# Whole modulation chunks, shift sums moved behind them, held-back sums lifted out at once, in a two-layer fp32 backbone

## The chip, the cores and the metric

The kernel runs on one core of one Trainium2 chip. The metric is the device time of one execution in microseconds, as the median of the runs: 2995.39 us over 3 runs (2994.27 to 2996.09).

## The reference, cut to what matters

Two layers work on 256 latent and 256 context tokens of width 2048, in fp32. Layer 0 mixes tokens by centred pooling, layer 1 by neighbourhood attention; behind each stands a gated MLP of inner width 5504 with a depthwise convolution of width 3. Only layer 0 up to its first MLP products is touched, and two norms later.

```python
def modulate(x, shift, scale):
    return x * (1 + scale) + shift

def conv_ffn(u, w_gate, w_up, conv_w, conv_b, w_down):
    gp = jnp.pad(u @ w_gate, ((0, 0), (1, 1), (0, 0)))
    gte = gp[:, :T] * conv_w[0] + gp[:, 1:T + 1] * conv_w[1] + gp[:, 2:] * conv_w[2] + conv_b
    return (jax.nn.silu(gte) * (u @ w_up)) @ w_down

def pool_mix(u, w, b, scale):          # 4 groups of 512 channels, windows 2, 4, 8, 16
    ...
    parts.append(window_sum / count[None, :, None] - ug)
    ...
    y = jnp.einsum('btgc,gcd->btgd', p, w).reshape(B, T, D) + b
    return y * scale
```

The shift, scale and gate of each sub-layer come from a product of SiLU(c) with a modulation matrix (2048 x 12288 a layer, for latent and context).

## The kernel before

**Precision.** Every fp32 weight tile is split into a high part (cast on ScalarE, line 172) and a low part (difference on VectorE, line 175); a product is three fp32r matmuls of 128x512, the 512 columns being both streams of 256 tokens.

**The four stages.** Layer 0 is worked in four groups g of 512 channels (lines 946 on). Stage g makes the first eight gate and up tiles (`cg`, `cu`) as far as the channels of group g go, while VectorE, GpSimd and ScalarE prepare the pooling mixer of group g + 1 and its products `pm` run on TensorE (PE). Tiles 0 to 5 are added up in SBUF (`part`, line 869). Tiles 6 and 7 stay in PSUM over all four stages (`HELD`); they must be multiplied by the RMS of the norm at the end (line 534, `late`), since the norm is known in stage 3 only.

**Modulation.** A chunk is 512 outputs of the modulation matrix. It has four groups of weights (2 loads of 512 KB each, `wm`) and 16 matmuls of 128x512 on 32 columns of the array (`tile_position`), line 216, which the trace has as 32 records. Chunks come in the order 4, 0, 8, 16, 12, and then 1 with 5, 9, 17, 13, the same with 2 and with 3. A generator yields after each group, and `need` (line 617) draws it on between and in the middle of the tiles. Two groups at a time are loaded and run (`run`, line 209), and the first matmul of each group of four waits for the last load so far ("whole steps"). When a chunk is done, ScalarE copies it out (`modev`, line 227), PE transposes it (`modt`, line 232) and VectorE sums it.

**Shift sums.** The shift of the modulation goes through the MLP weights apart: `early_shifts` (line 829) multiplies the raw weights of a tile pair by the shift vector, 8 matmuls of 128x256 on 32 columns (`pw`, line 838, 16 records), at the head of the first tile of each of the four weight loads of a stage. VectorE adds them up (line 847).

**Rooms and queues.** Loads are issued by SP's queue (line 151) in the order that the build gives them; a load that waits holds up those behind it. Each takes the next room of a ring (line 134): six rooms of its own pool and up to twelve that are lent by the activations (`lend`, line 130), the tiles `A4` to `A15` and under the same names `ph` (pooled activations) and `Ad` (scaled activations). The raw weights of a tile pair hold two rooms aside (`aside`, line 897), until their shift sum has run. PE too works in a written order, in which a scheduler has laid the program's instructions.

**The end of the four stages.** Behind stage 3 come `late` for tile 6, the normalised activations `A` 12 to 15 (line 469), and the first full pair of gate and up tiles `g`, `u` number 8 (lines 1026 to 1028).

**Later norms.** `Norm.each` (line 432) sums squares with matmuls into separate columns that VectorE adds (line 455); four matmuls whose result nobody reads stand behind them at one norm.

Of the kernel before, what the change touches and what calls it, by code (L numbers as in the profile page):

```python
# [17 lines left out]
P = 128  # L18
# [14 lines left out]
NS = 8  # L33
# [26 lines left out]
def kernel(ctx: ExitStack, tc: tile.TileContext, xT, cxT, wmod, wg, wu, wd, wp,  # L60
# [63 lines left out]

    hold = []

    RING = {"wst": 3, "wm": 2, "wa": 1}
# [32 lines left out]
    def split(ts, name, share=0, lows=None):  # L160

        parts = []
        for j, (t, n) in enumerate(ts):
            turn[0] += 1
            pools = [whp] * 3 + extra
            pool = pools[turn[0] % len(pools)]
            hi = pool.tile([P, 1024], F32R, tag="wh", name=f"{name}h{j}")
            lo = pool.tile([P, 1024], F32R, tag="wl", name=f"{name}l{j}")
            with ExitStack() as behind:
                for ins in hold:  # L170
                    behind.enter_context(tc.issue_after(ins))
                nc.scalar.copy(hi[:, :n], t[:, :n])  # L172
                eng = nc.gpsimd if share and turn[0] % share == 0 else nc.vector
                if lows is None:
                    eng.tensor_tensor(lo[:, :n], t[:, :n], hi[:, :n].bitcast(F32), op=ALU.subtract)  # L175
# [27 lines left out]
    copied = {}  # L203

    def mod_pe(chs, sc, pool):

        ps = bank("m", f"mod{chs[0]}")
        for c, ch in enumerate(chs):
            run = 1 if ch in (0, 4, 8, 12, 16) else 2
            for g in range(4):  # L210
                if g % run == 0:
                    tss = [load(lambda a, b: wmod[0, ch, e, :, a:b], 2048, f"wm0_{ch}_{e}") for e in range(g, g + run)]
                for e in range(g, g + run) if g % run == 0 else ():
# [164 lines left out]
    class Norm:  # L378
# [55 lines left out]
        def each(self, filler=None):  # L434

            with tc.high_priority():
                pairs = range(0, self.n // P, 2)
                sqs = [self.acc] + self.last
                na = len(sqs)
                ps = {i: bank("d", f"{self.name}s{i}") for i in pairs}  # L440
                todo = [(a, i) for a in range(na) for i in pairs]
                if len(pairs) == 2:
                    todo[3:5] = todo[4:2:-1]
                for a, i in todo:
                    for j in range(2):
                        ins = nc.tensor.matmul(ps[i][:, na * j + a : na * j + a + 1], sqs[a][:, P * (i + j) : P * (i + j) + P],
                                               ones, start=True, stop=True)
                self.last_sum = ins.ins
                vs = self.v = {}
                pbs = [bank("d", f"{self.name}b{i}") for i in pairs]  # L450
                if filler is not None:
                    unread(pbs[0], 4, filler[:, 0:P], filler[:, 0:512], self.last_sum)
                for i in pairs:
                    v = vs[i] = main.tile([P, 2], F32, name=f"{self.name}v{i}")
                    nc.vector.tensor_reduce(out=v, in_=ps[i][:, 0 : 2 * na].rearrange("p (j a) -> p j a", a=na), axis=AX.X,
                                            op=ALU.add)
                    self.diag = nc.vector.tensor_scalar(v, v, 1.0 / D, EPS, op0=ALU.mult, op1=ALU.add).ins
                    self.power(v)
                return [self.spread(vs[i], range(2), pb) for i, pb in zip(pairs, pbs)]
# [47 lines left out]
    with ExitStack() as ph0:  # L507
# [12 lines left out]
        PART = {}  # L520

        def late(f):

            res = []
            for q in range(2):
                if f < NC:
                    r = PART[f][:, q]
                    nc.gpsimd.tensor_tensor(r, r, late_norm[0], op=ALU.mult)
                else:
                    with ExitStack() as now:  # L530
                        if f == NC:
                            now.enter_context(tc.high_priority())
                        r = f0.tile([P, 512], F32, tag="t2", name=f"late{f}_{q}")
                        nc.vector.tensor_tensor(r, HELD[f, q], late_norm[0], op=ALU.mult)
                for s in both:
# [30 lines left out]
        with ExitStack() as phs:  # L566
# [319 lines left out]
            def partial(g, sh, between):  # L886

                step = 0
                c = 0
                for fa in range(0, NS, 4):  # L890
                    for q, (nm, wsrc) in enumerate((("g", wg), ("u", wu))):
# [7 lines left out]
                        for j in range(4):  # L899
                            f = fa + j  # L900
                            if (g, c) == (0, 0) and j < 2:
                                step += 1
                                continue
                            between(2 * step)
                            if j == (3 if fa == 0 and q == 0 else 0):
                                need(20 * g + 21)
                                assert g in READY
                                early_shifts(g, c, sh, ts)
                                rooms.extend([aside.pop(0), aside.pop(0)])
                            if f >= NC:  # L910
# [4 lines left out]
                            else:  # L915
                                ps = bank("d", f"c{nm}{g}_{f}")
                                first = final = True
                            tile_of(ps, parts, g, j, first, final, lambda: between(2 * step + 1))
                            step += 1
                            if f < NC:  # L920
                                put(ps, g, q, f)
                        c += 1
                        if g < 3 or q == 0:
                            continue
# [105 lines left out]
        def gu0(f):  # L1030
            res = []
            both_parts = []
            for nm, wsrc in (("g", wg), ("u", wu)):
                parts = ld(wsrc[0, f], f"w{nm}0_{f}")
                if f > NS:
                    pump()
                ps = bank("gu", f"{nm}0_{f}")
                gu_mm(ps, parts, range(12 if f == NS else KT))
                res.append(ps)
                both_parts.append(parts)  # L1040
            for ps, parts in zip(res, both_parts) if f == NS else ():
                gu_mm(ps, parts, range(12, KT))
            return res
# [46 lines left out]
        r6 = late(NC)  # L1090
        normalise(0, 3, h_of, both, rstd, f0, range(12, KT))
        res = gu0(NS)
        acts[NC], sg = gate0(NC, *r6)
# [44 lines left out]
    with ExitStack() as ph2:  # L1138
# [136 lines left out]

        n5 = Norm((0,), f1, "n5", 2)

        def down1(c, fs, acts, after=None):
            n = len(fs)
            last = c == len(chunks) - 1  # L1280
            for mg in range(4):
                parts = split(load(lambda a, b: wd[1, mg, :, fs[0] + a // 512 : fs[0] + b // 512, :], 512 * n, f"wd1_{c}_{mg}"),
                              f"wd1_{c}_{mg}")
                for m in range(4):
                    ps = bank("d", f"d1_{c}_{mg}_{m}")
                    for i in range(n):
                        hi, lo = parts[i // 2]
                        o = 512 * (i % 2) + P * m
                        if last:
                            nc.tensor.matmul(ps[:, :T], hi[:, o : o + P], acts[i][:, 0], start=(i == 0), stop=False)  # L1290
                            nc.tensor.matmul(ps[:, :T], hi[:, o : o + P], acts[i][:, 1], start=False, stop=False)
# [39 lines left out]
        with tc.issue_after(n5.done):  # L1331
            for k in range(KT - 6, KT):
                final_gain(k)
        rstd = n5.each()[0]
        rs = f1.tile([P, 512], F32, tag="t2", name="rs5")[:, 0:T]
# [392 lines left out]
```

## Time and profile before

| | |
|---|---|
| median of 3 runs | 2995.39 us (2994.27 to 2996.09) |
| profiled execution | 2992.32 us, its span 2990.5 us |
| mean granted TensorE clock | 0.998 of full speed |
| PE busy | 2946.3 us (99%), 14947 matmuls |
| VectorE / ScalarE / GpSimd busy | 2034.9 (68%) / 1353.7 (45%) / 869.7 us (29%) |
| chain that ended last | PE 87%, VectorE 5%, DMA 1%, ScalarE 1% |

Busy time is a share over the span. The stages that the change touches lie in the first 410 us; in the timelines there, a row is a stretch of equal matmuls, with its start, its time and the count, and in brackets how long the engine idled before it and what ended that.

### The profile page before, as it was taken

How to read it: one execution, taken by the hardware profiler on the slowest of the kernel's cores; microseconds unless marked ns; L12 is line 12 of the kernel's file. 1: busy time of each engine (PE TensorE's matmuls, PEld its weight loads, DVE VectorE, ACT ScalarE, POOL GpSimd, SP SyncE). 2: the span in 40 equal slices, each digit the busy share in tenths (PEclk: the TensorE clock that was granted, in tenths of full speed). 3: DMA queues.
4: the chain of work that ended last, by engine and by line, in shares of the span. 5: the costliest groups of instructions: out<-in, count | busy, mean ns of one | idle time of the engine just before them, and what ended most of it. 6: DMA issues, size and time to landing. Idle time of an engine off the chain costs nothing.

```text
span 2990.5 us, 41160 instructions
## 1 busy us (share of the span) xinstructions
PE 2946.3 (99%) x14947; PEld 2407.3 (80%) x14947; DVE 2034.9 (68%) x2910; ACT 1353.7 (45%) x2226; POOL 869.7 (29%) x861
## 2 busy tenths in 40 slices
PE   7999999999999999999999999999999999999998
PEld 4665778888888888888887888888788888888887
DVE  5465887657687867787777657474877666666666
ACT  4423562333323233332335434343556666566665
POOL 1111410311404031241421111010101665566665
PEclk9999999999999999999999999999999999999999
DMA  9988535545785866786772433333356565555553
GB/s 395 363 323 305 186 124 178 165 157 188 230 236 183 255 186 212 230 249 194 229 229 80 130 101 113 106 114 98 112 180 200 177 201 189 189 183 184 188 184 113
DMA packets 225069, 572.34 MB, mean 191 GB/s; under 512 B 55265, under 2 KB 68449, under 8 KB 224865
## 3 DMA queue, kind: packets, MB, share of 16 engines
q1 hardware_dynamic: 224864, 569.70, 59.0%
q8 instruction: 118, 1.93, 0.3%
q14 instruction: 87, 0.70, 0.1%
HBM read 563.32 MB, written 11.53 MB: 192 GB/s over the span
## 4 chain that ended last, share of the span: by engine, by line
PE 87%; DVE 5%; DMA 1%; issue 1%; ACT 1%; SPq 0%; POOL 0%; DVEq 0%; POOLq 0%; ACTq 0%
PE u L1222 5%; PE g L1222 5%; PE d L1065 5%; PE d L1064 5%; PE d L1063 5%; PE d L1294 5%; PE u L1028 4%; PE u L1027 4%; PE u L1026 4%; PE g L1028 4%; PE g L1027 4%; PE g L1026 4%; PE u L1229 3%; PE g L1229 3%; PE d L1298 3%; PE k L1445 2%
## 5 line engine op out<-in xcount | busy, mean ns | idle before, releaser
L1084 POOL TENSOR_TENSOR hl<-hl,dy 128x256 f32<-128x256 f32 x144 | 144.9, 1006 | 923.0 <-ACT dy L1081 664.3
L1311 POOL TENSOR_TENSOR hl<-hl,dy 128x256 f32<-128x256 f32 x320 | 313.6, 1011 | 232.6 <-ACT dy L1309 229.6
L308 DVE SCALAR_TENSOR_TENSOR macc<-wm,sc,macc 128x512 f32<-128x512 f32 x360 | 263.5, 783 | 8.3 <-DMA wm<-wmod 8.0
L286 DVE SCALAR_TENSOR_TENSOR macc<-wm,sc,macc 128x1024 f32<-128x1024 f32 x120 | 161.0, 1342 | 98.2 <-DMA wm<-wmod 97.3
L1081 ACT ACTIVATE dy<-d,modT 128x256 f32<-128x256 f32 x224 | 92.3, 470 | 114.6 <-PE d L1065 106.7
L1084 POOL TENSOR_TENSOR hc<-hc,dy 128x256 f32<-128x256 f32 x144 | 143.2, 994 | 0.0
L1309 ACT ACTIVATE dy<-d,modT 128x512 f32<-128x512 f32 x160 | 104.5, 683 | 57.4 <-PE d L1298 55.8
L1492 POOL COPY bias<-rows 128x160 f32<-128x160 f32 x64 | 39.7, 631 | 311.1 <-DVE nm L1501 180.6
L175 DVE TENSOR_TENSOR wd_3l<-wd,wd_3h 128x1024 fp32r<-128x1024 f32 (+1 forms) x44 | 56.7, 1293 | 78.8 <-ACT wd_3h L172 78.3
L550 ACT ACTIVATE sg<-g 128x512 f32<-128x512 f32 x43 | 27.3, 634 | 165.0 <-DVE g L547 165.0
L216 PE MATMUL mod<-wm,sc 128*32 128x512 f32 x640 | 86.8, 599 | 4.7 <-DMA wm<-wmod 3.2
L175 DVE TENSOR_TENSOR wd_2l<-wd,wd_2h 128x1024 fp32r<-128x1024 f32 (+1 forms) x44 | 58.2, 1333 | 43.7 <-ACT wd_2h L172 43.1
L644 POOL TENSOR_TENSOR pf<-ws,inv 128x256 f32<-128x256 f32 x28 | 23.4, 857 | 194.6 <-issue 93.1
L175 DVE TENSOR_TENSOR wd_1l<-wd,wd_1h 128x1024 fp32r<-128x1024 f32 (+1 forms) x44 | 54.4, 1241 | 35.5 <-ACT wd_1h L172 35.5
L172 ACT CAST wd_0h<-wd 128x1024 fp32r<-128x1024 f32 (+1 forms) x44 | 45.1, 1031 | 57.6 <-PE g L1027 45.6
L1065 PE MATMUL d<-act,wd_1l 128*128 128x512 f32 x172 | 67.1, 390 | 1.2 <-DVE wd_1l L175 1.2
L172 ACT CAST wd_3h<-wd 128x1024 fp32r<-128x1024 f32 (+1 forms) x44 | 45.3, 1031 | 50.0 <-PE u L1222 31.8
L172 ACT CAST wd_1h<-wd 128x1024 fp32r<-128x1024 f32 (+1 forms) x44 | 44.8, 1028 | 51.1 <-PE u L1222 28.3
L1063 PE MATMUL d<-act,wd_0h 128*128 128x512 f32 x172 | 66.5, 390 | 1.0 <-ACT dy L1081 1.0
L1063 PE MATMUL d<-act,wd_3h 128*128 128x512 f32 x172 | 67.3, 391 | 0.0
L1064 PE MATMUL d<-act,wd_2h 128*128 128x512 f32 x172 | 67.2, 391 | 0.0
L1065 PE MATMUL d<-act,wd_3l 128*128 128x512 f32 x172 | 67.1, 390 | 0.0
(1726 smaller groups left out, 9304.4 us busy)
## 6 DMA issues: line engine op xcount, KB each, us to landing
wm<-wmod SPq DMA_DIRECT2D x384, 512.0 KB, 6.2
wd<-wd SPq DMA_DIRECT2D x168, 512.0 KB, 4.4
wg<-wg SPq DMA_DIRECT2D x156, 512.0 KB, 4.5
wu<-wu SPq DMA_DIRECT2D x156, 512.0 KB, 4.7
wv<-wv SPq DMA_DIRECT2D x32, 512.0 KB, 3.9
wk<-wq SPq DMA_DIRECT2D x32, 512.0 KB, 3.8
wq<-wq SPq DMA_DIRECT2D x32, 512.0 KB, 3.7
wo<-wo SPq DMA_DIRECT2D x32, 512.0 KB, 4.4
```

Source lines behind the costliest of these rows:

```text
L175: eng.tensor_tensor(lo[:, :n], t[:, :n], hi[:, :n].bitcast(F32), op=ALU.subtract)
L308: nc.vector.scalar_tensor_tensor(acc[:, s], w, sc2[:, k, s : s + 1], acc[:, s], op0=ALU.mult, op1=ALU.add)
L1026: nc.tensor.matmul(ps, hi[:, c : c + P], xh, start=(k == 0), stop=False)
L1027: nc.tensor.matmul(ps, hi[:, c : c + P], xl, start=False, stop=False)
L1028: nc.tensor.matmul(ps, lo[:, c : c + P], xh, start=False, stop=(k == KT - 1))
L1063: nc.tensor.matmul(ps, hi[:, o : o + P], xh, start=(i == 0), stop=False)
L1064: nc.tensor.matmul(ps, hi[:, o : o + P], xl, start=False, stop=False)
L1065: nc.tensor.matmul(ps, lo[:, o : o + P], xh, start=False, stop=(i == n - 1))
L1084: nc.gpsimd.tensor_tensor(h_of(s)[:, k, :], h_of(s)[:, k, :], y[:, s], op=ALU.add)
L1222: ins = nc.tensor.matmul(ps, hi[:, c : c + P], flat(x[k]), start=(k == 0), stop=False)
L1229: nc.tensor.matmul(ps[:, T:], lo[:, c : c + P], x[k][:, 0], start=False, stop=(k == KT - 1))
L1311: nc.gpsimd.tensor_tensor(hl[:, k, :], hl[:, k, :], y[:, q], op=ALU.add)
```

## The change

Six things are done. A modulation chunk other than 0, 4, 8, 12, 16 is loaded and run as a whole (`run` 4, eight loads, 16 matmuls). A shift sum is put on a list when its tile begins, and runs behind the next modulation run, in stage 3 at once; the rooms of its raw weights go back to the ring then. The held sums of tile 6 are multiplied by the RMS right behind their own last tile. The first full gate/up pair splits its up weights in two halves and makes the last four `A` behind the first half. `Norm.each` adds in PSUM. Two fillers instead of four stand at one norm, and two are put into the last norm.

```diff
-            run = 1 if ch in (0, 4, 8, 12, 16) else 2
+            run = 1 if ch in (0, 4, 8, 12, 16) else 4
             for g in range(4):
                 if g % run == 0:
+                    fresh.append(ch)
                     tss = [load(lambda a, b: wmod[0, ch, e, :, a:b], 2048, f"wm0_{ch}_{e}") for e in range(g, g + run)]
...
-                        ins = nc.tensor.matmul(ps[i][:, na * j + a : na * j + a + 1], sqs[a][:, P * (i + j) : P * (i + j) + P],
-                                               ones, start=True, stop=True)
+                        ins = nc.tensor.matmul(ps[i][:, j : j + 1], sqs[a][:, P * (i + j) : P * (i + j) + P],
+                                               ones, start=(a == 0 and j == 0), stop=(a == na - 1 and j == 1))
...
-                    unread(pbs[0], 4, filler[:, 0:P], filler[:, 0:512], self.last_sum)
+                    unread(pbs[0], 2, filler[:, 0:P], filler[:, 0:512], self.last_sum)
...
-                    nc.vector.tensor_reduce(out=v, in_=ps[i][:, 0 : 2 * na].rearrange("p (j a) -> p j a", a=na), axis=AX.X,
-                                            op=ALU.add)
-                    self.diag = nc.vector.tensor_scalar(v, v, 1.0 / D, EPS, op0=ALU.mult, op1=ALU.add).ins
+                    self.diag = nc.vector.tensor_scalar(v, ps[i][:, 0:2], 1.0 / D, EPS, op0=ALU.mult, op1=ALU.add).ins
...
+        def lift(f, q):
+
+            r = f0.tile([P, 512], F32, tag="t2", name=f"late{f}_{q}")
+            nc.vector.tensor_tensor(r, HELD[f, q], late_norm[0], op=ALU.mult)
+            return r
...
+                def sum_shifts(half):
+
+                    if half is not None:
+                        fresh.clear()
+                        between(half)
+                    if waiting and (half is None or fresh or g == 3):
+                        early_shifts(*waiting.pop(0))
+                        rooms.extend([aside.pop(0), aside.pop(0)])
...
-                            between(2 * step)
                             if j == (3 if fa == 0 and q == 0 else 0):
                                 need(20 * g + 21)
                                 assert g in READY
-                                early_shifts(g, c, sh, ts)
-                                rooms.extend([aside.pop(0), aside.pop(0)])
+                                waiting.append((g, c, sh, ts))
+                            sum_shifts(2 * step)
...
-                            tile_of(ps, parts, g, j, first, final, lambda: between(2 * step + 1))
+                            tile_of(ps, parts, g, j, first, final, lambda: sum_shifts(2 * step + 1))
+                            if g == 3 and f == NC:
+                                with tc.high_priority():
+                                    lifted[q] = lift(f, q)
...
+                        if fa and q:
+                            while waiting:
+                                sum_shifts(None)
...
+        def gu0_first(f):
+            gate = ld(wg[0, f], f"wg0_{f}")
+            ts = load(lambda a, b: wu[0, f][:, a:b], 2048, f"wu0_{f}")
+            up = split(ts[:1], f"wu0_{f}_0")
+            res = [bank("gu", f"{nm}0_{f}") for nm in "gu"]
+            gu_mm(res[0], gate, range(12))
+            hold[:] = low
+            first_low = low[0]
+            up += split(ts[1:], f"wu0_{f}_1")
+            hold.clear()
+            with tc.issue_after(first_low):
+                normalise(0, 3, h_of, both, rstd, f0, range(12, KT))
+            gu_mm(res[1], up, range(12))
+            gu_mm(res[0], gate, range(12, KT))
+            gu_mm(res[1], up, range(12, KT))
             return res
...
-        normalise(0, 3, h_of, both, rstd, f0, range(12, KT))
-        res = gu0(NS)
+        res = gu0_first(NS)
...
-        rstd = n5.each()[0]
+        rstd = n5.each(final_hi[0])[0]
```

How the order moves on three engines is shown by pieces of the two builds.

SP's queue at the end of stage 0, before (`wm_13` are the loads of chunk 13, `wm_2` those of chunk 2, `wcg` and `wcu` the raw gate and up weights, `inv` a table of the mixer):

```order
L151 DMA wm_13_0_0_1290<-wmod 128x1024
L151 DMA wm_13_0_1024_1292<-wmod 128x1024
L151 DMA wm_13_1_0_1294<-wmod 128x1024
L151 DMA wm_13_1_1024_1296<-wmod 128x1024
L151 DMA wcg_0_0_1339<-wg 128x2x512
L151 DMA wcg_0_1024_1341<-wg 128x2x512
L151 DMA wm_13_2_1024_1360<-wmod 128x1024
L151 DMA wm_13_2_0_1358<-wmod 128x1024
L151 DMA wm_13_3_0_1362<-wmod 128x1024
L669 DMA inv_1661<-inv 128x256
L151 DMA wm_13_3_1024_1364<-wmod 128x1024
L151 DMA wm_2_2_0_1454<-wmod 128x1024
```

The same twelve places of SP's queue after the change:

```order
L675 DMA inv_1667<-inv 128x256
L152 DMA wm_2_0_0_1407<-wmod 128x1024
L152 DMA wm_2_0_1024_1409<-wmod 128x1024
L152 DMA wcu_0_0_1467<-wu 128x2x512
L152 DMA wcu_0_1024_1469<-wu 128x2x512
L152 DMA wm_6_0_0_1500<-wmod 128x1024
L152 DMA wm_6_0_1024_1502<-wmod 128x1024
L152 DMA wm_13_0_0_1280<-wmod 128x1024
L152 DMA wm_13_0_1024_1282<-wmod 128x1024
L152 DMA wm_13_1_0_1284<-wmod 128x1024
L152 DMA wm_13_1_1024_1286<-wmod 128x1024
L152 DMA wm_13_2_0_1288<-wmod 128x1024
```

The loads of chunk 13 now stand behind two each of chunk 2, of the next up weights and of chunk 6.

PE in the middle of stage 0, before (`mod` is a modulation matmul with its weights `wm_chunk_group`, `modt` its transposes, `pw` a shift sum, `cg` and `cu` the gate and up tiles):

```order
L851 MATMUL cg_1029<-Ad_593,wcg_4l_892 128x512
L216 MATMUL mod_924<-wm_9_2_0_983,sc 32x512 x2
L216 MATMUL mod_924<-wm_9_2_1024_985,sc 32x512 x2
L216 MATMUL mod_924<-wm_9_3_0_987,sc 32x512 x2
L216 MATMUL mod_924<-wm_9_3_1024_989,sc 32x512 x2
L232 MATMUL modt_1036<-ident,modev_1027 128x128 x4
L216 MATMUL mod_1044<-wm_17_0_0_1045,sc 32x512 x2
L216 MATMUL mod_1044<-wm_17_0_1024_1047,sc 32x512 x2
L216 MATMUL mod_1044<-wm_17_1_0_1049,sc 32x512 x2
L216 MATMUL mod_1044<-wm_17_1_1024_1051,sc 32x512 x2
L838 MATMUL pw_3_1094<-wcu_4_0_1082,sh_233 32x256
L851 MATMUL cu_4_1104<-Ad_573,wcu_4h_1086 128x512 x2
```

The same place of PE after the change:

```order
L220 MATMUL mod_904<-wm_9_3_0_917,sc 32x512 x2
L220 MATMUL mod_904<-wm_9_3_1024_919,sc 32x512 x2
L236 MATMUL modt_1026<-ident,modev_1017 128x128 x4
L844 MATMUL pw_2_1082<-wcg_4_0_873,sh_233 32x256
L844 MATMUL pw_2_1082<-wcg_4_1024_875,sh_233 32x256
...
L220 MATMUL mod_1034<-wm_17_0_0_1035,sc 32x512 x2
L220 MATMUL mod_1034<-wm_17_0_1024_1037,sc 32x512 x2
L220 MATMUL mod_1034<-wm_17_1_0_1039,sc 32x512 x2
L220 MATMUL mod_1034<-wm_17_1_1024_1041,sc 32x512 x2
```

The halves of chunks 9 and 17, with products of `cg` between those of 9 and of `cu` behind the first half of 17, have become two whole chunks with the transposes and a shift sum between them.

VectorE at the end of stage 3, before (`nrm` and `A` make the normalised activations, `late_0` is the gate half of tile 6, `wg_8l` the low half of the first full gate weights):

```order
L480 SCALAR_TENSOR_TENSOR A_0_3_3101<-nrm_3102,modT_14_2106,A_0_3_3101 128x256 x2
L847 TENSOR_TENSOR shlast<-shlast,pw_3_3182 128x512
L175 TENSOR_TENSOR wg_8l_3316<-wg_8_0_3311,wg_8h_3315 128x1024
L547 SCALAR_TENSOR_TENSOR g_1_3139<-part_634,vt,g_1_3139 128x2x255
L869 TENSOR_TENSOR part_947<-part_947,cu_4_3192 128x512
L559 TENSOR_TENSOR act_3049<-sg_3046,act_3049 128x512
L469 SCALAR_TENSOR_TENSOR nrm_3174<-hl,modT_18_1990,n2acc 128x256
L469 SCALAR_TENSOR_TENSOR nrm_3174<-hc,modT_18_1990,n2acc 128x256
L469 SCALAR_TENSOR_TENSOR nrm_3207<-hl,modT_18_1990,n2acc 128x256
L534 TENSOR_TENSOR late_0_3271<-cg_999,n2acc 128x512
L469 SCALAR_TENSOR_TENSOR nrm_3207<-hc,modT_18_1990,n2acc 128x256
```

VectorE at that place after the change:

```order
L471 SCALAR_TENSOR_TENSOR nrm_3077<-hc,modT_17_1275,n2acc 128x256
L875 TENSOR_TENSOR part_987<-part_987,cg_5_3087 128x512
L471 SCALAR_TENSOR_TENSOR nrm_3102<-hl,modT_18_1980,n2acc 128x256
L471 SCALAR_TENSOR_TENSOR nrm_3102<-hc,modT_18_1980,n2acc 128x256
L527 TENSOR_TENSOR late_0_3122<-cg_989,n2acc 128x512
L471 SCALAR_TENSOR_TENSOR nrm_3125<-hl,modT_18_1980,n2acc 128x256
L471 SCALAR_TENSOR_TENSOR nrm_3125<-hc,modT_18_1980,n2acc 128x256
L176 TENSOR_TENSOR wcu_4l_3172<-wcu_4_1024_3165,wcu_4h_3171 128x1024
L557 TENSOR_TENSOR sg_3046<-sg_3046,part_632 128x512
```

`late_0` has moved up, before the two `nrm` that precede the low half of the up weights.

## Rows read from the trace of the kernel before

**Rows 1.** Windows view, two stretches: us, busy, PEclk, DMA share, GB/s
```profile
40.00:90.00 50.00, 48.85 (x294) 27.27 (x293) 24.52 (x48) 22.41 (x43) 4.07 (x5) 1.00 1.03 418
323.70:410.00 86.30, 81.40 (x409) 63.78 (x406) 79.74 (x122) 59.10 (x113) 29.84 (x25) 0.98 0.49 161
```

**Rows 2.** The timeline of PE at 98 to 151 us: start, us, what
```profile
98.81 0.61 PE L851 MATMUL cu<-Ad,wcu_0h 128*128 128x512 f32 x2
99.35 1.92 PE L216 MATMUL mod<-wm,sc 128*32 128x512 f32 x16
101.20 0.51 PE L851 MATMUL cu<-Ad,wcu_0l 128*128 128x512 f32 x1
101.55 0.64 PE L851 MATMUL cu<-Ad,wcu_0h 128*128 128x512 f32 x2
...
102.35 1.92 PE L216 MATMUL mod<-wm,sc 128*32 128x512 f32 x16
...
106.29 1.21 PE L851 MATMUL cg<-Ad,wcg_4h 128*128 128x512 f32 x4
...
150.89 3.64 PE L216 MATMUL mod<-wm,sc 128*32 128x512 f32 x32
```

**Rows 3.** PE's waits over the span: for what, us, times, longest
```profile
PE modt L232 <- ACT modev L227: 4.1, 5, 1.2
...
PE g L1026 <- DVE late L534: 2.1, 1, 2.1
PE v L1370 <- ACT A L475: 1.6, 1, 1.6
...
PE cg L851 <- ACT Ad L819: 0.6, 1, 0.6
```

**Rows 4.** The timelines of PE and of SP's queue at 115 to 117 us
```profile
115.21 1.92 PE L216 MATMUL mod<-wm,sc 128*32 128x512 f32 x16
...
116.31 0.82 SPq L151 DMA_DIRECT2D wp<-wp  x2
```

**Rows 5.** The source view, line 151, 116.2 to 117.9 us: ns, starts, landing
```profile
L151 SPq DMA_DIRECT2D wm<-wmod x2: 381/385/389, 117.2 to 117.7; - x2
...
DMA to landing us min/median/max: 4.0/5.3/6.5
```

**Rows 6.** The source view, line 151 in 100.3 to 105.3 us
```profile
L151 SPq DMA_DIRECT2D wm<-wmod x8: 328/392/926, 100.4 to 105.0; - x8
...
DMA to landing us min/median/max: 5.1/8.5/10.4
```

**Rows 7.** The timeline of PE at 378 to 391 us
```profile
379.00 0.60 PE L927 MATMUL pt<-ident,shlast 128*128 128x128 f32 x4
381.71 0.50 PE L1026 MATMUL g<-A,wg_8h 128*128 128x512 f32 x1 [2.11 <-DVE late L534]
...
382.29 0.60 PE L1028 MATMUL g<-A,wg_8l 128*128 128x512 f32 x1
...
385.67 0.42 PE L1027 MATMUL g<-A,wg_8h 128*128 128x512 f32 x1
...
389.81 0.39 PE L1027 MATMUL g<-A,wg_8h 128*128 128x512 f32 x1
390.03 0.39 PE L1028 MATMUL g<-A,wg_8l 128*128 128x512 f32 x1
```

**Rows 8.** The windows view, of two stretches behind waits of PE
```profile
383.00:384.00 1.00, 1.00 (x4) 0.71 (x4) 1.00 (x2) 0.54 (x2) 1.00 (x2) 0.50 0.00 0
1628.70:1632.00 3.30, 3.27 (x14) 2.70 (x15) 3.30 (x7) 1.98 (x5) 0.00 (x0) 1.00 0.00 0
```

**Rows 9.** The timeline of VectorE at 1622 us
```profile
1622.65 0.16 DVE L455 TENSOR_REDUCE n3v<-n3s 128x2 f32<-128x6 f32 x1 [1.41 <-PE n3s L446]
```

**Rows 10.** The timeline of PE in the first 42 us
```profile
9.90 6.28 PE L580 MATMUL warm<-n1q,ident 128*128 128x256 f32 x18 [0.71 <-ACT n1q L391]
...
40.32 1.89 PE L376 MATMUL pm<-hl,ident 128*128 128x256 f32 x8
```

More of the change, by code (lines that the diff above doesn't have):

```diff
@@ L125 @@
     hold = []
+    low = []
     RING = {"wst": 3, "wm": 2, "wa": 1}
@@ L174, in split @@
                 if lows is None:
-                    eng.tensor_tensor(lo[:, :n], t[:, :n], hi[:, :n].bitcast(F32), op=ALU.subtract)
+                    low[:] = [eng.tensor_tensor(lo[:, :n], t[:, :n], hi[:, :n].bitcast(F32), op=ALU.subtract).ins]
                 else:
@@ L203 @@
     copied = {}
+    fresh = []
     def mod_pe(chs, sc, pool):
@@ L443, in each @@
                     todo[3:5] = todo[4:2:-1]
+                pbs = [bank("d", f"{self.name}b{i}") for i in pairs]
                 for a, i in todo:
                     for j in range(2):
-                        ins = nc.tensor.matmul(ps[i][:, na * j + a : na * j + a + 1], sqs[a][:, P * (i + j) : P * (i + j) + P],
-                                               ones, start=True, stop=True)
+                        ins = nc.tensor.matmul(ps[i][:, j : j + 1], sqs[a][:, P * (i + j) : P * (i + j) + P],
+                                               ones, start=(a == 0 and j == 0), stop=(a == na - 1 and j == 1))
                 self.last_sum = ins.ins
                 vs = self.v = {}
-                pbs = [bank("d", f"{self.name}b{i}") for i in pairs]
                 if filler is not None:
-                    unread(pbs[0], 4, filler[:, 0:P], filler[:, 0:512], self.last_sum)
+                    unread(pbs[0], 2, filler[:, 0:P], filler[:, 0:512], self.last_sum)
                 for i in pairs:
                     v = vs[i] = main.tile([P, 2], F32, name=f"{self.name}v{i}")
-                    nc.vector.tensor_reduce(out=v, in_=ps[i][:, 0 : 2 * na].rearrange("p (j a) -> p j a", a=na), axis=AX.X,
-                                            op=ALU.add)
-                    self.diag = nc.vector.tensor_scalar(v, v, 1.0 / D, EPS, op0=ALU.mult, op1=ALU.add).ins
+                    self.diag = nc.vector.tensor_scalar(v, ps[i][:, 0:2], 1.0 / D, EPS, op0=ALU.mult, op1=ALU.add).ins
                     self.power(v)
@@ L520 @@
         PART = {}
+        def lift(f, q):
+            r = f0.tile([P, 512], F32, tag="t2", name=f"late{f}_{q}")
+            nc.vector.tensor_tensor(r, HELD[f, q], late_norm[0], op=ALU.mult)
+            return r
+        lifted = {}
         def late(f):
@@ L529, in late @@
                 else:
[L530 to L534, printed above, removed]
+                    r = lifted[q] if f == NC else lift(f, q)
                 for s in both:
@@ L889, in partial @@
                 c = 0
+                waiting = []
+                def sum_shifts(half):
[5 more added lines that the diff above has]
+                        rooms.extend([aside.pop(0), aside.pop(0)])
                 for fa in range(0, NS, 4):
@@ L1031, in gu0 @@
             res = []
-            both_parts = []
             for nm, wsrc in (("g", wg), ("u", wu)):
                 parts = ld(wsrc[0, f], f"w{nm}0_{f}")
-                if f > NS:
-                    pump()
+                pump()
                 ps = bank("gu", f"{nm}0_{f}")
-                gu_mm(ps, parts, range(12 if f == NS else KT))
+                gu_mm(ps, parts, range(KT))
                 res.append(ps)
-                both_parts.append(parts)
-            for ps, parts in zip(res, both_parts) if f == NS else ():
-                gu_mm(ps, parts, range(12, KT))
+            return res
+        def gu0_first(f):
[13 more added lines that the diff above has]
+            gu_mm(res[1], up, range(12, KT))
             return res
@@ L1276 @@
         n5 = Norm((0,), f1, "n5", 2)
+        final_hi = []
         def down1(c, fs, acts, after=None):
@@ L1289, in down1 @@
                         if last:
+                            final_hi[:] = [hi]
                             nc.tensor.matmul(ps[:, :T], hi[:, o : o + P], acts[i][:, 0], start=(i == 0), stop=False)
```

## The prediction, made before the changed kernel was run

> **What bounds the kernel now.** I read four views, in this order. First the busy time of the engines by stretch: TensorE (PE) computes 48.85 of 50 us from 40 to 90 us and 81.40 of 86.3 from 323.7 to 410 [rows 1]; the whole change lies in the first 410 us but for two small edits, and there the time is what PE does in its written order. The same rows show the loads at the full rate of the queue early on (DMA share 1.03, 418 GB/s: a load of 512 KB each 1.25 us) and VectorE nearly full late (79.74 of 86.3 us). Second the timeline of PE, for what an entry into the narrow 128x32 matmuls costs [rows 2]. Third the list of waits, for what PE loses [rows 3]. Fourth the issue and landing of loads, since the change makes a chunk wait for its last load [rows 4 to 6].
>
> **Entries saved.** 16 records of `mod` take 1.92 us and 32 take 3.64, so a record is 0.107 and a chunk 3.64 [rows 2]. The run of 16 at 99.35 holds PE until 101.20, 0.14 more than 16 x 0.107; about 0.09 goes before it and 0.12 behind it: 0.35 per entry. From 102.35 to 106.29 two runs that end inside a group of four stand: 3.94 us for 16 x 0.107 + 16 x 0.053 + two products of 0.23, so 0.9 and the outer edges 0.2, 0.55 each. By the order PE enters the narrow matmuls 46 times from 68 us on, 12 of them cut in a group; after the change 29 times, 4 of them cut. 8 x 0.55 + 9 x 0.35 = 7.5 us less; bounds 6 and 9 (taking every entry at 0.35 or at 0.55).
>
> **Waits that go.** PE waits five times for `modev`, 4.1 us together [rows 3]. Of those behind chunks 9, 18 and 12 the one of 18 (1.2, the longest) should go, since `modev` of 18 no longer stands behind a cast on ScalarE; but the transposes of chunks 9 and 10 now stand directly behind their chunks, so two of about 0.75 stay or come. The 0.6 for `Ad` [rows 3] is hidden by a shift sum that now stands before it. Together 1.0 less (0 to 2).
>
> **Early exit.** Before the first full gate tile PE has its last work at 379.00 and the tile starts at 381.71, after 2.1 us for `late` [rows 3, 7]. Then it runs at half clock from 382.29 to 385.67 (0.50 granted [rows 8]): 8 matmuls in 3.38 us that take 0.22 each at full clock (389.81 to 390.03) [rows 7], 1.6 lost. 3.7 us are to be had. VectorE is full there [rows 1]; the order puts `late` before two `nrm` and not away, and the low halves and `A` 10 to 15 come as late as before, so the next late thing is VectorE's. I take 3, bounds 1 and 4.7 (all of it, and 1 us of VectorE's lag on the up tile behind it, by estimate). The reductions of the later norms (0.16 and a step each [rows 9]) give 0.2 at n3 and n5 each, nothing at n4, where work covers them; fillers stand in waits: 0.4 (0 to 0.6).
> Gains: 7.5 + 1.0 + 3.0 + 0.4 = 11.9 us.
>
> **What whole chunks cost.** The first matmul of a whole chunk now waits for the last of its eight loads; the order on PE is fixed, so all behind it waits too. A load needs a room, and SP issues in its written order. The half run of `mod` starts at 115.21 and SP issues the load into its first freed room at 116.31, 1.1 later [rows 4]. Four loads issued there from 116.3 to 117.7 land from 4.0 to 6.5 after their issue: the first at start + 5.1, the fourth at 117.7 + 6.5 = 124.2, start + 9.0 [rows 5]. Eight issued from 100.4 to 105.0 land up to 10.4 later: the eighth 15.0 after the first issue [rows 6]; at the queue's 1.25 it would be 4.0 + 7 x 1.25 = 12.8.
> - Chunk 17 stands behind chunk 9, the transposes of 9 and a shift sum: PE comes to it at start of 9 + 3.6 + 0.75 + 1.55 (estimate for transposes and sums, from the column times) = 5.9. Its last four loads use the rooms of chunk 9's first four: start + 9.0. Wait 3.1 to 5, taken 3.5.
> - Chunk 18 behind 10 likewise, but six loads: start + 9.0 + 2 x 1.25 = 11.5, up to 12.6. Wait 5.6 to 6.7, taken 6.2.
> - Chunk 19 behind 11: seven products stand between, so PE comes at 6.8. Wait 4.7 to 5.8, taken 5.3.
> - Chunk 13: SP's order shows its eight loads behind two loads each for `wm_2`, `wcu` and `wm_6`. The latter four take the memory of `Ad` 0 to 3, which the last up tile reads to its end; `wm_13_0_0` itself has the memory of `ph5`, read last in the mixer's last tile. All eight are thus issued when PE has only six products, four transposes and a shift sum left, 3.1 us from the start of the releasing product. Eighth landing: 0.4 + 12.8 to 15.0. Wait 10.1 to 12.3, taken 11.2. In the kernel before, the loads of 13 stood ahead of those of 2.
> - Chunk 1: its loads come at the queue's full pace [rows 1], so the shift sum moved from before it (1.1 us) only makes PE early: 0 to 1.1, taken 0.8.
> Together 27.0 (23.5 to 31). Chunks 5, 2, 6, 10, 3, 7, 11, 14, 15 I find covered: there 10 to 20 us of tiles stand between release and use.
>
> **The clock behind a long wait.** The wait of 2.1 was followed by half clock [rows 7, 8]; that of 1.6 for `A` in the second layer [rows 3] was not: 1.00 granted behind it [rows 8]. At the start PE idles 8 us and the 18 `warm` matmuls behind it take 6.28 (0.35 each), where 8 of the same shape take 1.89 later (0.22) [rows 10]. All four waits are over 3 us, so I count 1.6 for each: 6.4, bounds 0 and 7.
> The Trainium skill, page "TensorE: Matmul & The Clock Gate" (Why this matters for your kernels), tells to leave no long idle gaps between bursts of matmuls, because the clock then goes back to its lower level. By that rule the sum keeps the 6.4; without it the time is 3010. The rows here show it once in mid-kernel and once at the start.
> The Trainium skill, page "DMA: Bandwidth & Descriptors" (Where 436 GB/s comes from), has loads from HBM bound by about 358 GB/s. The rows here show 418, so page and trace differ and the trace decides; by the page the eight loads of chunk 13 would take 1.5 us more, six loads 1 more, and the time would be 3020.
>
> **Sum.** -11.9 + 27.0 + 6.4 = 21.5 us. The profiled execution took 2992.3 (span 2990.5), so 3013.8; the median of the runs is 2995.4, 3.1 above it, so I write 3016.
>
> **Rivals.**
> A. Waits as above, no half clock: 2995.4 + 15.1 = 3010. For it: a wait of 1.6 brought none. Against: 2.1 did.
> B. The loads come 4 us sooner than I read at each place (the shortest landing is 4.0, so rooms would have to be free that much earlier). Chunk 17 waits 0, 13 7.2, 18 2.2, 19 1.3, chunk 1 0.8: 11.5, with half clock behind one, 1.6: 2995.4 + 1.2 = 2997, no change. For it: one landing mode, seen only behind half runs. Against: the order of PE and SP is written, and each wait is a difference of two sums of rows.
> C. Not slower but faster: the chunk's loads are there in time, because rooms are freed earlier than their last readers as I read them. The place is SP between the first mixer and chunk 13; it decides when `wm_13` is issued before the last up tile, over 12 us earlier, and the pairs 9/17, 10/18, 11/19 have their rooms from older tiles. Then only the gains stand: 2983.5. For it: from 40 to 90 us PE lost 1.15 us, with the queue full [rows 1]. Against: the names in SP's order.
> D. Only chunk 13 is late, since its order is plain: 2995.4 - 11.9 + 11.2 + 1.6 = 2996.
>
> **How the numbers follow.** Forecast with half clock 0.58; A 0.18; B and D 0.12; C 0.12. Forecast and A are slower by over 0.2% (6 us, about what a measurement of this kernel tells from no change): 0.76, and 0.02 of B and D that end beyond it: 0.78; same 0.10; faster 0.12. Within the forecast the low ends give 2995.4 - 14.5 + 23.5 + 5 = 3009, the high ends 2995.4 - 8 + 31 + 7 = 3025; A reaches down to 3004. The range 2995 to 3026 takes in most of B and D and leaves out C and a little at both ends.
>
> **What would show it.** Right: `mod` waits for `wm` four times for 3 to 12 us between 115 and 320, the longest near 150 to 165, with granted clock 0.5 behind them; SP waits at that place for the mixer's products; PE enters the narrow matmuls 29 times; no wait of 2 us before the first full gate tile. Wrong: if the loads of chunk 13 are issued while the last up tile runs and land before PE comes, or if PE waits for `wm` under 12 us in all, the forecast falls.

## The result, and the profile after

The changed kernel takes 3023.26 us (median of 4 runs, 3019.99 to 3026.01), the kernel before 2995.74 (4 runs): a ratio of 1.0093, 95% interval 1.0081 to 1.0106. It is 27.5 us slower; 20.6 had been forecast. The profiled execution took 3026.01 (span 3024.2), the longest of the four, and that of before, 2992.32, lies below all other runs of it, so the two traces stand 33.7 apart and not 27.5.

The list of PE's waits over the whole span, after (for what, us, times, longest), against [rows 3]:

```profile
PE mod L220 <- DMA wm<-wmod: 29.3, 11, 13.3
PE warm L586 <- ACT n1q L395: 8.7, 2, 8.1
PE mod L220 <- issue: 4.2, 2, 3.9
PE modt L236 <- ACT modev L231: 3.7, 5, 0.8
...
PE cg L857 <- ACT Ad L825: 2.5, 2, 1.8
PE d L1097 <- ACT hc L1112: 2.3, 1, 2.3
```

Waits for `wm` now stand first (before, there were 3.2 us of them, all in the first 40 us), and one for `hc` is new. The wait for `late` is gone. The timeline of PE, after, shows where the first kind falls (start, us, what, and in brackets the idle time before it):

```profile
116.56 3.64 PE L220 MATMUL mod<-wm,sc 128*32 128x512 f32 x32
...
126.49 5.34 PE L220 MATMUL mod<-wm,sc 128*32 128x512 f32 x32 [3.88 <-issue]
...
168.57 6.55 PE L220 MATMUL mod<-wm,sc 128*32 128x512 f32 x32 [13.30 <-DMA wm<-wmod]
...
231.82 5.65 PE L220 MATMUL mod<-wm,sc 128*32 128x512 f32 x32 [6.33 <-DMA wm<-wmod]
...
322.45 6.41 PE L220 MATMUL mod<-wm,sc 128*32 128x512 f32 x32 [5.42 <-DMA wm<-wmod]
```

These are chunks 17, 13, 18 and 19, the four that were named. Together 28.9 us of waiting; and where an undisturbed chunk takes 3.64 (the row at 116.56, as in [rows 2]), they take 5.34, 6.55, 5.65 and 6.41: 9.4 us more, spent at half clock (0.50 granted). The windows view of after (us, busy of PE, PEld, DVE, ACT, POOL, then PEclk, DMA share, GB/s) has it in and behind the longest wait, and below it the stretch before that:

```profile
40.00:90.00 50.00, 48.24 (x274) 27.50 (x273) 24.52 (x48) 21.60 (x41) 4.08 (x5) 1.00 1.03 418
...
166.00:168.00 2.00, 0.00 (x0) 0.00 (x0) 0.00 (x0) 0.00 (x0) 0.00 (x0) 0.50 1.04 406
170.00:174.00 4.00, 4.00 (x24) 1.13 (x20) 3.18 (x6) 4.00 (x7) 0.00 (x0) 0.50 0.21 37
```

PE, VectorE and ScalarE all stand still from 166 to 168 while the queue runs full (share 1.04): PE waits for loads that were issued late. The first row answers to [rows 1] and is as before. The source view of the loads (ns, starts, landing) at 152 to 158 us, after, against [rows 6]:

```profile
L152 SPq DMA_DIRECT2D wm<-wmod x8: 328/520/1455, 152.5 to 157.5; - x8
...
  PE mod L220: 13.3, 1
...
DMA to landing us min/median/max: 7.2/9.9/10.9
```

The eight loads of chunk 13 start in one burst at 152.5, and the last lands at 157.5 + 10.9 = 168.4. What held them up stands in the list of the waits of SP's queue from 143 to 160 us, after:

```profile
SPq L152 <- PE cu L857: 7.5, 4, 5.8
...
SPq L152 <- PE pm L669: 1.0, 1, 1.0
```

SP first waits for the last up tile (`cu`), for the loads that stand ahead of chunk 13, and then for the mixer's last product (`pm`), both as the prediction had read them from the order.

The first full gate/up pair and what follows it, timeline of PE, after, against [rows 7]:

```profile
411.53 0.60 PE L949 MATMUL pt<-ident,shlast 128*128 128x128 f32 x4
411.89 0.47 PE L1048 MATMUL g<-A,wg_8h 128*128 128x512 f32 x1
...
434.12 0.39 PE L1097 MATMUL d<-act,wd_0h 128*128 128x512 f32 x1
...
447.44 0.73 PE L1097 MATMUL d<-act,wd_1h 128*128 128x512 f32 x1 [2.28 <-ACT hc L1112]
447.97 0.63 PE L1098 MATMUL d<-act,wd_1h 128*128 128x512 f32 x1
```

From `pt` to the first down product `d` it is 22.6 us where it was 27.2 (379.00 to 406.23): the early exit gains 4.6, the whole of it. Eleven microseconds later PE waits 2.28, and its products behind that come at half pace (0.63 a row, where 0.39 is usual [rows 7]). ScalarE's timeline, after, shows what it waited for:

```profile
443.84 1.04 ACT L173 CAST wd_2h<-wd 128x1024 fp32r<-128x1024 f32 x1
445.41 0.63 ACT L556 ACTIVATE sg<-g 128x512 f32<-128x512 f32 x1 [0.53 <-DVE g L553]
445.95 0.91 ACT L543 ACTIVATE late<-late,wsh 128x256 f32<-128x256 f32 x2
446.77 0.35 ACT L1112 COPY hl<-d 128x256 f32<-128x256 f32 x1
447.02 0.37 ACT L1112 COPY hc<-d 128x256 f32<-128x256 f32 x1
```

The copies that empty the first down bank stand behind a silu and two activations for a later tile; PE, now earlier, has all four banks full and must wait. At 449.75 us of before (481.83 of after) the distance between the traces is 32.1, at the first `d` it was 27.9: 4.2 of the 4.6 are given back.

### The profile page after: what moved, and what is told of

It is laid out like the page before. It is cut to its first block, busy times and chain, and to the rows that moved or that the text cites. A ratio compares the mean times of both kernels' runs of the same rounds, so it can differ in the third digit from the quotient of the medians.

```text
span 3024.2 us, 41115 instructions
## 1 busy us (share of the span) xinstructions
PE 2949.3 (98%) x14947; PEld 2411.4 (80%) x14947; DVE 2038.4 (67%) x2906; ACT 1355.6 (45%) x2226; POOL 869.7 (29%) x861
## 4 chain that ended last, share of the span: by engine, by line
PE 83%; DVE 4%; DMA 2%; issue 1%; ACT 1%; SPq 0%; POOL 0%; DVEq 0%; ACTq 0%
PE g L1255 5%; PE u L1255 5%; PE d L1329 5%; PE d L1097 5%; PE d L1099 5%; PE d L1098 5%; PE g L1050 4%; PE u L1050 4%; PE u L1049 4%; PE g L1049 4%; PE g L1048 4%; PE u L1048 4%; PE u L1262 3%; PE g L1262 3%; PE d L1333 3%; PE k L1480 2%
## 5 line engine op out<-in xcount | busy, mean ns | idle before, releaser
L556 ACT ACTIVATE sg<-g 128x512 f32<-128x512 f32 x43 | 27.2, 633 | 164.0 <-DVE g L553 163.9
L220 PEld LDWEIGHTS mod<-wm,sc 128*32 128x32 f32 x640 | 21.8, 119 | 87.4 <-issue 58.4
L1097 PE MATMUL d<-act,wd_1h 128*128 128x512 f32 x172 | 67.7, 394 | 2.3 <-ACT hc L1112 2.3
L1098 PE MATMUL d<-act,wd_1h 128*128 128x512 f32 x172 | 67.6, 393 | 0.0
```

Source lines behind the costliest of these rows:

```text
L1097: nc.tensor.matmul(ps, hi[:, o : o + P], xh, start=(i == 0), stop=False)
L1098: nc.tensor.matmul(ps, hi[:, o : o + P], xl, start=False, stop=False)
```

## The experiments

Theory A, made from the two orders: a whole chunk asks for eight rooms at once, and a shift sum that runs behind a modulation run keeps the two rooms of its raw weights out of the ring while those eight are handed out; chunk 13 then gets the room of `ph5`. Theory W: whole chunks are late by themselves. Each time stands against runs of the kernel before on the same chip (2993.3 to 2993.9).

**Whole chunks alone**

```diff
 (kernel before)
-            run = 1 if ch in (0, 4, 8, 12, 16) else 2
+            run = 1 if ch in (0, 4, 8, 12, 16) else 4
```

> The kernel before with one edit: chunks run whole (run 4), the shift sums stay at the head of their tiles. Theory A (two causes together: a whole chunk needs eight rooms, and a shift sum moved behind a run keeps two rooms of raw weights out of the ring while those eight are handed out): here the loads of chunk 13 take rooms that chunks 9 and 17 free, so chunk 13 does not wait; chunk 17 has two late loads instead of four and waits 0.5 to 1.5 us; 18 and 19 have 26 and 28 products between and do not wait. Entries into the narrow matmuls fall from 43 to 28 from the first gate tile on: 6 to 7 us less. Time 2988 to 2992. Theory W (whole chunks are late by themselves): four waits of 3 to 12 us as in the changed kernel, 3010 or more.

Measured: 2994.0 us, ratio 0.9998 (0.9989 to 1.0007). W falls: 28 us of loss are not there. Chunk 17 waits 1.42, 13, 18 and 19 not at all. The time lies 2 us over the range that A gave; the gain does not show in the median. The list of PE's waits from 40 to 480 us has new small ones:

```profile
PE modt L232 <- ACT modev L227: 4.6, 6, 0.9
PE u L1028 <- DVE wu_8l L175: 2.3, 1, 2.3
...
PE mod L216 <- issue: 1.4, 1, 1.4
PE cg L851 <- DVE Ad L820: 1.3, 2, 0.7
```

`wu_8l` was 0.7 before, `Ad` 0.6: PE came earlier, VectorE did not. The waits alone don't account for the median: this trace is of the shortest of the 11 runs (2989.57), and in it PE is still 3.6 us ahead of before at the first full gate tile (378.08 against 381.71) and 2.0 at the first `d` (404.23 against 406.23). Why the other runs don't keep that stays open.

**The changed kernel, shift sums back at the head of their tiles**

```diff
 (changed kernel)
+                            between(2 * step)
                             if j == (3 if fa == 0 and q == 0 else 0):
...
-                                waiting.append((g, c, sh, ts))
-                            sum_shifts(2 * step)
+                                early_shifts(g, c, sh, ts)
+                                rooms.extend([aside.pop(0), aside.pop(0)])
```

> The changed kernel with the shift sums back at the head of their tiles; whole chunks, early exit and the norms stay. Theory A: no wait for a chunk over 1.5 us before 320 us, 34 to 38 us less than the changed kernel. If the 4.6 us of the early exit are given back by the wait for the copies of the first down products, the time is that of whole chunks alone, 2988 to 2992; if they stay, 2984 to 2986. Theory W: 3010 or more.

Measured: 2991.3 us, ratio 0.9991 (0.9982 to 1.0000). Moving the sums back, and with them the moment when their rooms go back to the ring, takes 32 us away (30 by the distances to the kernel before on each chip), a little less than the 34 to 38 expected; nothing else differs from the changed kernel. The time fits a gain of the early exit that is given back: PE waits 2.28 for `hc` here too. Chunk 17 waits 1.77, over the 1.5 that A allowed, with half clock behind it. SP's timeline of this kernel has the loads of chunk 13 early, from 120.29 on, where they take rooms that chunks 9 and 17 give back:

```profile
119.08 1.12 SPq L152 DMA_DIRECT2D wp<-wp  x2
120.29 6.52 SPq L152 DMA_DIRECT2D wm<-wmod  x6
129.14 0.33 SPq L675 DMA_DIRECT2D inv<-inv  x1
129.56 1.44 SPq L152 DMA_DIRECT2D wm<-wmod  x2
```

and chunk 13 starts at 151.84, with no wait.

**Rooms held back, sums at the head**

```diff
 (the kernel of the last experiment)
-                            between(2 * step)
...
-                                rooms.extend([aside.pop(0), aside.pop(0)])
+                                waiting.append(c)
+                            sum_shifts(2 * step)
...
                     if waiting and (half is None or fresh or g == 3):
-                        early_shifts(*waiting.pop(0))
+                        waiting.pop(0)
                         rooms.extend([aside.pop(0), aside.pop(0)])
```

> Whole chunks, early exit and norms as in the changed kernel, the shift sums at the head of their tiles as before, but the two rooms of their raw weights go back to the ring as late as in the changed kernel (behind the next modulation run). Theory A (rooms held back): by SP's order chunk 13 again starts with the room of ph5 and has its eight loads behind the last mixer products, 17 has three late loads and 18 and 19 six; waits of about 3, 13, 7 and 4 us with half clock behind them, 3012 to 3024. Rival P (it is the place of the shift sums on TensorE that matters, not the rooms): the time of the kernel with the sums at the head, 2989 to 2993.

Measured: 3024.0 us, ratio 1.0097 (1.0083 to 1.0111). Up to chunk 13 PE's order in the trace is that of the last kernel, sum for sum; only the moment when two rooms are handed back differs, and the waits are there again. (Behind chunk 13 the scheduler has laid some sums at other places, but none between 10 and 18 or between 11 and 19.) PE's timeline:

```profile
125.71 6.05 PE L220 MATMUL mod<-wm,sc 128*32 128x512 f32 x32 [4.44 <-issue]
...
168.81 4.98 PE L220 MATMUL mod<-wm,sc 128*32 128x512 f32 x32 [12.97 <-DMA wm<-wmod]
...
231.84 5.89 PE L220 MATMUL mod<-wm,sc 128*32 128x512 f32 x32 [7.37 <-DMA wm<-wmod]
...
322.01 5.18 PE L220 MATMUL mod<-wm,sc 128*32 128x512 f32 x32 [2.91 <-DMA wm<-wmod]
```

The rival (the place of the sums on PE) falls: with the rooms held back the time is that of the changed kernel (3023.26), wherever the sums stand. So the held rooms make whole chunks late, and whole chunks without them are not late. Whether halves would be late too with the rooms held back is the next question.

**Four chunks in halves, sums still moved**

```diff
 (changed kernel)
-            run = 1 if ch in (0, 4, 8, 12, 16) else 4
+            run = 1 if ch in (0, 4, 8, 12, 16) else 2 if ch in (13, 17, 18, 19) else 4
```

> The changed kernel with chunks 13, 17, 18 and 19 alone in halves again (the shift sums stay moved). Theory A: by SP's order the first half of chunk 13 still stands behind the last read of ph5, four loads instead of eight behind it, so it waits 3 to 6 us; the others wait under 3; with 9 entries more (4 us) the time is 2998 to 3008. Theory W: halves take the waits away altogether, 2990 to 2994.

Measured: 3007.2 us, ratio 1.0040 (1.0025 to 1.0056). Inside the range of A. Chunk 13 still waits 6.84, a little over the 3 to 6 expected, with half clock behind it (6.46 for its 32 records); the other waits for `wm` are 0.73 and 1.68. A wait for `modev` ahead of chunk 17 has grown from 0.73 to 3.21, also with half clock behind it (3.64 for 16 records that otherwise take 1.92). So the held rooms make a half chunk late as well, at least with the other chunks whole.

**Work in place of the four waits**

```diff
 (changed kernel)
+    FILL = {17: 4, 13: 15, 18: 7, 19: 6}
...
+                if g == 0 and ch in FILL:
+                    for _ in range(FILL[ch]):
+                        nc.tensor.matmul(ps, ident, sc[:, 0:512], start=True, stop=True)
```

> The changed kernel with matmuls whose result nobody reads ahead of chunks 17, 13, 18 and 19 (4, 15, 7 and 6 of 128x512 in f32, 0.85 us each by the f32 matmuls of 256 columns), so that TensorE works instead of waiting; the loads land when they did. If the half clock behind the four waits comes from idling, the four chunks run in 3.6 us instead of 5.3 to 6.6 and the time is 9 us shorter: 3012 to 3016. If the clock falls for another reason (the narrow matmuls, the loads), the time stays at 3021 to 3026.

Measured: 3016.8 us, ratio 1.0076 (1.0062 to 1.0089), 6.4 under the changed kernel, 0.8 above the range of the first case and clear of that of the second. Timeline of PE of this kernel, chunk 17, and its windows view behind the refilled waits of 13 and 19:

```profile
121.73 3.60 PE L221 MATMUL mod<-sc,ident 128*128 128x512 f32 x8
125.26 1.09 PE L849 MATMUL pw<-wcg,sh 128*32 128x256 f32 x16
126.97 3.64 PE L225 MATMUL mod<-wm,sc 128*32 128x512 f32 x32 [0.61 <-DMA wm<-wmod]
```

```profile
167.00:171.00 4.00, 3.54 (x32) 1.13 (x32) 2.00 (x3) 2.39 (x5) 0.00 (x0) 1.00 0.61 195
...
317.80:321.80 4.00, 3.93 (x34) 1.45 (x35) 3.68 (x6) 3.09 (x5) 0.28 (x1) 1.00 0.99 299
```

All four chunks run in 3.64 at 1.00, so the half clock came from idling. The Trainium skill, page "TensorE: Matmul & The Clock Gate" (Why this matters for your kernels), warns of such gaps; the trace agrees (0.50 granted behind the waits of the changed kernel, 1.00 where they are filled). Behind chunk 19 this trace is 7.3 us ahead of that of the changed kernel (321.44 against 328.79 for the next tile). Then 3.6 of it are lost again: a wait for `Ad` of 1.29 us, 0.73 in the changed kernel, has half clock behind it. (Behind this wait come two full products and then sixteen of one column; in the changed kernel eight full ones come first. Whether the wait alone brings the half clock is not shown.) The timeline row and the windows view there:

```profile
349.72 0.73 PE L862 MATMUL cg<-Ad,wcg_0h 128*128 128x512 f32 x2 [1.29 <-ACT Ad L830]
```

```profile
350.00:355.00 5.00, 5.00 (x24) 4.33 (x24) 3.16 (x10) 2.54 (x7) 1.02 (x1) 0.63 1.08 383
355.00:360.00 5.00, 5.00 (x17) 3.99 (x16) 0.00 (x0) 0.00 (x0) 0.00 (x0) 0.68 1.05 379
```

**The early exit: alone, and with the copies ahead.** Theory G: what it gains is given back, because ScalarE copies the first down products late. Both kernels here have early exit and norms, halves, sums at the head.

```diff
 (second one: on ScalarE, the two stand behind the first copy)
-                nc.scalar.activation(v, v, AF.Identity, bias=wsh[...])
+                with behind_copy(f == NS - 1):          # tc.issue_after(the first hc copy)
+                    nc.scalar.activation(v, v, AF.Identity, bias=wsh[...])
...
+            with behind_copy(f == 5):
                 nc.scalar.activation(sg, flat(g1), AF.Silu)
```

> The kernel before with the early exit and the norms alone: chunks in halves, shift sums at the head. Theory G: 4.6 us gained ahead of the first down products, and 4.1 given back by the wait of 2.3 for hc with half clock behind it: 2992 to 2995. Rival: the gain stays, since in halves ScalarE has more time, 2988 to 2991.

> The same with the copies of the first down products ahead on ScalarE. Theory G: 4 to 5 us under the kernel with early exit and norms alone, 2987 to 2990; against whole chunks with the same (2985.3) it shows what whole chunks are worth when no chunk is late: 2 to 5 us. If whole chunks save nothing, 2984 to 2986.

Measured: 2991.0 (0.9989, 0.9981 to 0.9998) and 2990.3 us (0.9988, 0.9979 to 0.9997). The first is at the edge of the rival's range and below that of G: 2.4 us are gained. Both are under the kernel before, but the second by no clear step under the first: 0.7 where G gave 4 to 5. The wait for `hc` did fall, from 2.24 to 0.31, but in the first kernel no half clock followed the 2.24 (1.00 granted from 415 to 417), as it did in the changed kernel (0.50 from 448 to 450), so only 2 us were to be had.

**Whole chunks, sums at the head, copies ahead**

```diff
 (the kernel with the sums at the head, and behind_copy as above)
```

> Whole chunks with the shift sums at the head, early exit and norms, and on ScalarE the copies of the first down products placed ahead of one silu and the two late activations that stood before them. Theory G (the early exit's gain is given back because these copies come late on ScalarE): the wait for hc of 2.3 us falls under 1, the half clock behind it goes, 2987 to 2989. Rival V (VectorE and ScalarE as a whole are behind by then, so another wait takes its place within 20 us): 2990 to 2993, with a wait of 2 us for act, wd or another copy before 470 us.

Measured: 2985.3 us, ratio 0.9976 (0.9966 to 0.9985); the wait for `hc` is 0.33. That is 2 us below the range of G; V falls. Of the 6 us against the sums at the head alone, 2 are that wait; in the profiles some 3 more are two half clocks (behind `hc`, and behind chunk 17: a wait of 1.77 there had it, this one of 1.46 does not; nothing in the edit touches that place, so this part is the chance of the two executions). Against the same kernel in halves (2990.3) whole chunks are 5 us ahead, but the other two pairs show nothing: 2994.0 against 2993.9, and 2991.3 against 2991.0 with early exit and norms in both. What whole chunks are worth by themselves lies between 0 and 5 us.

**The same, chunk 17 in halves**

```diff
-            run = 1 if ch in (0, 4, 8, 12, 16) else 4
+            run = 1 if ch in (0, 4, 8, 12, 16) else 2 if ch == 17 else 4
```

> The kernel with the copies first, and chunk 17 alone in halves. The wait of 1.8 us ahead of chunk 17 and the 1.7 us of half clock behind it go, two entries at 0.35 and 0.55 come back: 2.6 us under the kernel with the copies first, 2984 to 2987 by theory G, 2987 to 2990 by rival V. This would be the first version clearly under the kernel before.

Measured: 2982.3 us, ratio 0.9963 (0.9951 to 0.9976), 2 us below the range that G gave and the lowest median of all: 11 us under the kernel before and 41 under the changed one. The interval still overlaps that of the last kernel, so the step of 3 us between the two is not certain. Its list of PE's waits from 40 to 480 us has none for `wm`:

```profile
PE modt L236 <- ACT modev L231: 4.2, 5, 0.9
PE cg L863 <- DVE Ad L832: 1.3, 2, 0.7
PE cg L863 <- DVE part L881: 1.2, 1, 1.2
PE pm L672 <- ACT pz L821: 0.4, 2, 0.2
PE d L1104 <- ACT hc L1119: 0.3, 1, 0.3
```

## Why the prediction was right

The direction, the four places and the way that the time is lost there (loads issued late, PE waiting, half clock behind) were right, and the time lay 7 us over the forecast and inside the range. What in the change makes the loads late was wrong: the prediction charged it to whole chunks, and the runs show the held rooms. Term by term, from the two traces:

| term | forecast | measured |
|---|---|---|
| wait of chunk 17 | 3.5 | 3.9 |
| wait of chunk 13 | 11.2 | 13.3 |
| wait of chunk 18 | 6.2 | 6.3 |
| wait of chunk 19 | 5.3 | 5.4 |
| wait of chunk 1 | 0.8 | 0.6 |
| half clock behind the four | 6.4 | 9.4 |
| `modev`, `Ad` | -1.0 | +0.7 |
| entries | -7.5 | about -7.6 |
| early exit | -3.0 | -4.6, then +4.2 |

The measured terms add up to 31.6; the medians are 27.5 apart. The traces are the longest of the runs after and the shortest of before, so some 4 us of the column don't show in the medians.

- **The waits.** The three pairs came out within 0.4 us. PE reached chunk 17 at 6.1 behind the start of chunk 9 (forecast 5.9), and its last load landed at 9.8 (9.0); for chunk 18 it was 6.1 and 12.3 (5.9, and 11.5 to 12.6). Chunk 13 was mis-sized by 2.1: its burst took 152.5 to 168.4, 15.9 us, where 12.8 to 15.0 had been given with 0.4 ahead, because the first of the eight took 7.2 to land ([rows 6] had 5.1 as its shortest) and the other seven came 1.25 apart behind it. The load ahead of it had landed at 155.4; from there to 159 the queue moved 172 to 365 GB/s (windows of 1 us) and from 160 on 418. Why it was slow for those microseconds stays open.
- **The half clock** was sized by one place with a wait of 2.1 [rows 7]. Behind waits of 3.9 to 13.3 the slow stretch cost 1.7 to 2.9, not 1.6, and not more behind the longer wait in each case (2.8 behind 5.4, 2.0 behind 6.3). This term was sized 3.0 too low. Rival A, without half clock, fell.
- **The entries** can only be had as a rest: at `pt` the traces differ by 32.5, the waits make 28.9 + 0.6, the clock 9.4, `modev` and `Ad` 0.7 (3.5 to 2.3, 0.6 to 2.5), other small waits 0.5; 40.1, so 7.6 were saved elsewhere. The traces count 43 entries before and 27 after from the first gate tile to `pt` (46 and 29 were read from the order). That the rest is the entries is not shown: whole chunks against halves gave 0, 0 and 5 us in the medians.
- **`Ad`.** That a shift sum would hide its wait was wrong: PE waited 1.78 and 0.73 for it.
- **The early exit** is a step whose end was missed. The gain itself was the full 4.6, past the 3.0 that was taken out of care for VectorE. What the prediction had not looked for is what is late next: it looked at VectorE on the up tile, and the next wait was ScalarE's copies, 11 us further on, with half clock behind. Net 0.4; alone, with the norms and without the half clock, it came to 2.4 in the medians (2991.0).
- **The norms** can't be told from the spread: between 450 us and the end the traces of the changed kernel and of its variants drift against before by -2.2 to +2.6 us, with the same norms in all.
- **One thing that the prediction did not say.** It charged the waits to whole chunks ("What whole chunks cost"), with the moved sums as a mere change of place. It came out near because it took rooms and loads from the order of the changed build, in which the effect of the held rooms stands without its name. The experiments show the cause: whole chunks alone cost nothing (2994.0), rooms held back with whole chunks cost all 33 us (2991.3 to 3024.0), and with the four chunks in halves the held rooms still leave a wait of 6.84, in a time 13 over before (3007.2). The kernel with all chunks in halves and the sums moved was not run.
- **Two slips in its sums.** The sum of 21.5 on the median gives 3016.9, where 3016 is written. And the ends of its range take gains of 14.5 and 8, where its own bounds add up to 16.3 and 7: 3008 to 3026 instead of 3009 to 3025. Neither changes how it compares with 3023.

Rivals B, C and D fell with the four waits.

## What to carry to other kernels

When the unit of a load gets bigger, count the rooms that are free at that moment, not in all: whatever holds a room longer in the same edit (here two raw weight tiles until a sum has run) decides which old tenant the next load waits for, and SP's order beside the last reader of each room tells it before any run, but not which part of the edit has done it: for that, one part has to be taken back at a time. A wait of several microseconds on TensorE was paid twice here, once as idle time and again as half clock (28.9 and 9.4 us). And a gain ahead of an engine that is nearly full is only kept if the queue of the next engine is in the order in which the faster one will ask; here moving two activations behind one copy took the wait from 2.24 to 0.31.

## What the runs showed of the hardware

- The half clock is granted during the wait already (0.50 at 166 to 168 us with PE, VectorE, ScalarE and GpSimd idle) and stays for a while when work is back (0.50 at 170 to 174, 1.00 at 176 to 178). Waits of much the same length went either way. Without half clock behind them: 1.42 and 1.46 ahead of chunk 17, 1.6 in the second layer [rows 3, 8], 1.78 for `Ad` (changed kernel), 2.05 for `late` (whole chunks alone), 2.24 for `hc` (early exit alone). With it: 1.77 ahead of chunk 17, 2.11 for `late` [rows 7, 8], 2.24 for `hc` (four chunks in halves), 2.28 for `hc` (changed kernel). Where it came behind these, the slow clock cost 1.6 to 1.9 us, so one execution and the next, or a small shift of the order, can differ by that much.
- In the burst of eight loads of chunk 13 the landing times were 1.2 to 1.3 us apart with the engines idle (162.2, 163.4, 164.7, 165.9, 167.1, 168.4), the same 1.25 as in [rows 1] with all of them at work: here the queue's pace did not depend on them.
